# Down-products over a sliding set of eight experts, one shared PSUM rotation, and early low parts on GpSimd

## The chip, the cores and the metric

The kernel runs on one core of one Trainium2 chip. The metric is the device time of one execution in microseconds; lower is better. The time before is the median of three runs.

## What is computed

One residual block on 512 tokens of width 2048, in float32: RMSNorm, two causal attentions (stick-breaking and forgetting) with gated branches and an output projection, then a PEER layer (each token picks, for each of 8 heads, 16 of 16384 single-neuron experts by product keys), then a last RMSNorm. Cut to what matters here:

```python
h = rms_norm(x, norm_ffn_gain)
# expert_ids (t,h,k) and gates (t,h,k) from top-k over two sets of 128 sub-keys
u_sel = expert_u[idb]
act = jax.nn.gelu(jnp.einsum('thkd,td->thk', u_sel, xb))
w = gb * act
v_sel = expert_v[idb]
out = jnp.einsum('thk,thkd->td', w, v_sel)
x = x + out
return rms_norm(x, norm_final_gain)
```

## The kernel before

Matrix products keep float32 accuracy with three passes: `wload` (L96) loads a 128x2048 block of weights in two halves of 512 KB through SP's queue (L104, tile `wr`), ScalarE rounds each half to a high part `wh` (L109), and a low part `wl = wr - wh` is made on VectorE or GpSimd (L111). `mm3` (L117) then issues wh·ah (L118), wh·al (L119) and wl·ah (L120). `wh` and `wl` have three buffers each, `wr` four in the PEER part. From the PEER part on (where the list `more` is not empty) the first half's low part is made on VectorE and the second half's on GpSimd.

The attention part, to about 1335 us of the profile, is not touched. The PEER part treats tokens in two ways. For the last 192 tokens the chosen rows of `expert_u` and `expert_v` are gathered by indirect DMA, 1 MB a gather, by GpSimd's queue (L558), and reduced on VectorE (L565, L574, L582); the tile `row` has three buffers. The other 320 tokens (TD) are dense: the kernel multiplies by all 16384 experts, as 128 blocks of 128, which the code calls experts, and weighs the result with a gate matrix that is zero where an expert was not chosen.

The dense work on one expert c has three parts:

- `expert_up(c)` (L533): 48 matmuls of 320 columns with `uT[c]` into PSUM (`psu`), a scaling on VectorE (L537) and a gelu on ScalarE (L540), giving `gl`.
- `weigh(c)` (L825): `gl` times the gates `gg` of this expert (L830, VectorE), then high part (L833, ScalarE) and low part (L834, VectorE) in `wg`.
- the down-products (L845 to L859): groups of GC = 8 experts. For each of 8 column blocks `jb` a block of `vP` is loaded; each of its two 128-column parts takes 24 matmuls over the eight experts into one PSUM tile (`psy`), which VectorE adds to `acc` (L859).

The stages of this part, by the profile's clock:

- Selection, 1335 to about 2107 us: query projections, top-k on VectorE (`choose`), and the scatter that builds the gate matrix (L796, L801, L803) and stores it to DRAM (`gsp`). In between `early` (L626) runs the first NS = 53 experts' up-products and stores their `gl` to DRAM (`gact_sp`).
- Main, from 2107 us: groups 0 to 15. Experts 0 to 52 are fetched back from `gact_sp` (L815), so groups 0 to 5 have down-products alone; from expert 53 on each group has eight up-products and then its down-products. `gates(grp)` (L818) loads the 20x128 gates of a group's experts from `gsp` to `gg`, which has one buffer (it lies in the unused columns of `h2`).
- End: last norm and the stores.

Gathers are spread by `pace`: every up-product and every down-block counts one unit, and a list `todo` of 388 gathers and small steps is worked off at `rate` of them a unit. PSUM: tag `pu` (2 banks: `psu`, `psq2`), tag `px` (2 banks: `psy`, `psgt` and others), `pr` (4 banks, held by the gathers). The order on each engine is set by a scheduler from the program order and its own costs; it is fixed before the run.

```python
second = more and s == 1
ins = (nc.gpsimd if second else nc.vector).tensor_tensor(lo, raw, hi.bitcast(F32), op=ALU.subtract)
```

Of the kernel before, what the change touches and what calls it, by code (L numbers as in the profile page):

```python
# [18 lines left out]
P = 128  # L19
# [13 lines left out]
NG = NK // GC  # L33
# [10 lines left out]
NS = NH * UPS + TD // TB - -(-(TD // TB) // 3)  # L44
SLOW = 1.1
QROWS = 0.75
LEAD = 1
# [4 lines left out]
def block_kernel(ctx, tc, xT, gains, w_vf, bf, w_qk, w_v, w_g, w_br, w_o, w_q, keysT, uT, vP, expert_u, expert_v, outT):  # L52
# [38 lines left out]
    more = []  # L91
# [4 lines left out]
    def wload(src, between=None, pace=None, units=0.5):  # L96
# [3 lines left out]
        for s in range(2):  # L100
# [9 lines left out]
            second = more and s == 1  # L110
# [381 lines left out]
    pu = pool("pu", 2, space=PSUM)  # L492
    px = pool("px", 2, space=PSUM)
# [39 lines left out]
    def expert_up(c, pace=None):  # L533
        ps = pu.tile([P, T], F32, tag="pu", name="psu")
# [91 lines left out]
    def early(n, pace=None):  # L626
        for _ in range(n):
            if len(started) < NS:
                c = len(started)
                nc.scalar.dma_start(gact_sp[c], expert_up(c, pace))  # L630
                started.append(c)

    with ExitStack() as s1:
# [93 lines left out]
        for h in range(NH):  # L727
            sc = []
            sv = se.tile([P, 2, HT, NK], F32, tag="sv", name="sv")
            for p in range(2):  # L730
# [5 lines left out]
                ps = pu.tile([P, T], F32, tag="pu", name="psq2")  # L736
# [74 lines left out]
    def fetch(c):  # L811
        if c >= NS:
            return expert_up(c, pace)
        g = gl.tile([P, TD], F32, tag="gl", name="gl")
        nc.sync.dma_start(g, gact_sp[c])  # L815
        return g
# [6 lines left out]
    ahead = []  # L823

    def weigh(n):  # L825

        while len(ahead) < min(n + 1 + LEAD, NK):
            ahead.append(fetch(len(ahead)))
        g = ahead[n]
        nc.vector.tensor_tensor(g.rearrange("p (b t) -> p b t", t=TB), g.rearrange("p (b t) -> p b t", t=TB),  # L830
                                gg[:, :, n % GC], op=ALU.mult)
        wg = ex.tile([P, 2, TD], F32R, tag="wg", bufs=GC + 1, name="wg")
# [3 lines left out]

    gates(0)
    ws = [weigh(0)]
    assert len(started) == NS
    rate[0] = len(todo) / (2 * NK - NS - 8)  # L840
    for grp in range(NG):
        first = []
        while len(ws) < GC:
            ws.append(weigh(grp * GC + len(ws)))
        for jb in range(KC // JJ):  # L845
            w = wload(vP[grp, jb])
            if grp + 1 < NG and jb == 1:
                gates(grp + 1)
            if grp + 1 < NG and jb == KC // JJ - 2:
                first.append(weigh((grp + 1) * GC))  # L850
            for jj in range(JJ):
                j = jb * JJ + jj
                ps = px.tile([P, T], F32, tag="px", name="psy")
                for c in range(GC):
                    b = jj * GC + c
                    wh, wl = w[b // 8]
                    cc = slice(b % 8 * P, (b % 8 + 1) * P)
                    mm3(ps[:, :TD], wh[:, cc], wl[:, cc], ws[c][:, 0], ws[c][:, 1], c == 0, c == GC - 1)
# [86 lines left out]
```

## Time and profile before

| what | value |
|---|---|
| median of 3 runs | 3826.57 us (3822.14 to 3833.91) |
| profiled execution, its own time | 3835.57 us |
| its span, first to last instruction | 3833.9 us |
| mean granted TensorE clock | 0.968 |
| PE / PEld busy | 3555.4 us (93%) / 3242.6 us (85%) |
| DVE busy | 2650.1 us (69%) |
| ACT busy | 1274.8 us (33%) |
| POOL busy | 1168.8 us (30%) |
| HBM read, written | 848.69 MB, 35.96 MB |

A busy PE is not PE at its peak: matmuls overlap in the pipeline, so the row of a stretch is read by its number of matmuls as well. The shares are means over stages with different limits; the sections below read the stages apart. 1.7 us of the profiled time lie outside the span.

### The profile page before, as it was taken

How to read it: one execution, taken by the hardware profiler on the slowest of the kernel's cores; microseconds unless marked ns; L12 is line 12 of the kernel's file. 1: busy time of each engine (PE TensorE's matmuls, PEld its weight loads, DVE VectorE, ACT ScalarE, POOL GpSimd, SP SyncE). 2: the span in 40 equal slices, each digit the busy share in tenths (PEclk: the TensorE clock that was granted, in tenths of full speed). 3: DMA queues.
4: the chain of work that ended last, by engine and by line, in shares of the span. 5: the costliest groups of instructions: out<-in, count | busy, mean ns of one | idle time of the engine just before them, and what ended most of it. 6: DMA issues, size and time to landing. Idle time of an engine off the chain costs nothing.

```text
span 3833.9 us, 52828 instructions
## 1 busy us (share of the span) xinstructions
PE 3555.4 (93%) x20665; PEld 3242.6 (85%) x20665; DVE 2650.1 (69%) x3856; ACT 1274.8 (33%) x1798; POOL 1168.8 (30%) x766
## 2 busy tenths in 40 slices
PE   9999999999999999988988888889889999998997
PEld 7888888888887878788978778889889989898997
DVE  5333455434555349999699877788888788778886
ACT  4334222222223223344455322223333333333333
POOL 0000000000000013344522345555555545555552
PEclk9999999999999999998999999999999999999999
DMA  4222222222224236677866899899999999989993
GB/s 144 77 78 77 97 94 97 88 88 78 94 94 137 94 128 228 218 272 264 323 249 236 297 345 337 323 353 360 337 349 358 348 351 367 346 328 347 356 378 133
DMA packets 238249, 888.12 MB, mean 232 GB/s; under 512 B 22696, under 2 KB 79272, under 8 KB 186288
## 3 DMA queue, kind: packets, MB, share of 16 engines
q1 hardware_dynamic: 169792, 447.15, 33.5%
q0 software_dynamic: 58848, 425.75, 28.8%
q10 hardware_dynamic: 9360, 11.83, 0.8%
q8 instruction: 163, 2.67, 0.3%
q14 instruction: 86, 0.70, 0.1%
HBM read 848.69 MB, written 35.96 MB: 231 GB/s over the span
## 4 chain that ended last, share of the span: by engine, by line
PE 61%; DVE 18%; DMA 12%; issue 4%; ACT 2%; POOL 1%; SPq 1%; DVEq 0%; POOLq 0%; ACTq 0%
PE psy L118 5%; PE psy L119 4%; PE psy L120 4%; PE psg L120 3%; PE psg L119 3%; PE psg L118 3%; PE psq L120 3%; PE psq L119 3%; PE psu L120 3%; PE psq L118 3%; DVE wl L111 3%; PE psu L118 3%; PE psu L119 3%; DVE row L565 2%; DMA h<-gsp 2%
## 5 line engine op out<-in xcount | busy, mean ns | idle before, releaser
L109 ACT ACTIVATE wh<-wr 128x1024 fp32r<-128x1024 f32 x768 | 812.4, 1059 | 1919.5 <-PE psy L119 426.5
L111 DVE TENSOR_TENSOR wl<-wr,wh 128x1024 fp32r<-128x1024 f32 x496 | 622.4, 1255 | 457.6 <-ACT wh L109 455.4
L111 POOL TENSOR_TENSOR wl<-wr,wh 128x1024 fp32r<-128x1024 f32 x272 | 658.8, 2422 | 447.9 <-ACT wh L109 348.2
L120 PE MATMUL psu<-h,wl 128*128 128x320 f32 x2048 | 645.8, 316 | 91.2 <-DVE wl L111 91.0
L118 PE MATMUL psy<-wg,wh 128*128 128x320 f32 x2048 | 647.1, 317 | 73.3 <-ACT wg L833 38.1
L120 PE MATMUL psy<-wg,wl 128*128 128x320 f32 x2048 | 645.4, 315 | 15.7 <-DVE wl L111 15.7
L119 PE MATMUL psy<-wg,wh 128*128 128x320 f32 x2048 | 647.0, 316 | 12.3 <-DVE wg L834 12.3
L118 PE MATMUL psu<-h,wh 128*128 128x320 f32 x2048 | 645.8, 315 | 12.5 <-DVE gl L537 7.0
L119 PE MATMUL psu<-h,wh 128*128 128x320 f32 x2048 | 643.3, 314 | 0.0
L120 PEld LDWEIGHTS psu<-h,wl 128*128 128x128 f32 x2048 | 395.2, 193 | 104.8 <-DVE wl L111 104.3
L118 PEld LDWEIGHTS psy<-wg,wh 128*128 128x128 f32 x2048 | 395.0, 193 | 81.6 <-ACT wg L833 39.8
L120 PEld LDWEIGHTS psy<-wg,wl 128*128 128x128 f32 x2048 | 395.8, 193 | 18.5 <-DVE wl L111 18.3
L118 PEld LDWEIGHTS psu<-h,wh 128*128 128x128 f32 x2048 | 395.0, 193 | 18.5 <-ACT wh L109 12.1
L119 PEld LDWEIGHTS psy<-wg,wh 128*128 128x128 f32 x2048 | 395.6, 193 | 15.6 <-DVE wg L834 15.6
L119 PEld LDWEIGHTS psu<-h,wh 128*128 128x128 f32 x2048 | 395.0, 193 | 0.0
L582 DVE SCALAR_TENSOR_TENSOR accg<-row,gact,accg 128x2048 f32<-128x2048 f32 x127 | 298.0, 2347 | 27.3 <-DMA row<-ev,idx 27.0
L565 DVE SCALAR_TENSOR_TENSOR row<-row,rstd_t,h2g 128x2048 f32<-128x2048 f32 x128 | 299.0, 2337 | 10.3 <-DMA row<-eu,idx 10.3
L558 POOL DMA_INDIRECT row<-eu,idx x128 | 159.1, 1243 | 320.2 <-DVE row L565 165.6
L118 PE MATMUL psq<-h,wh 128*128 128x512 f32 x512 | 205.4, 401 | 8.3 <-ACT wh L109 8.3
L558 POOL DMA_INDIRECT row<-ev,idx x128 | 148.7, 1162 | 209.1 <-DVE accg L582 181.7
L119 PE MATMUL psq<-h,wh 128*128 128x512 f32 x512 | 206.2, 403 | 0.4 <-DVE h L169 0.4
L120 PE MATMUL psq<-h,wl 128*128 128x512 f32 x512 | 205.6, 402 | 0.1
(310 smaller groups left out, 6089.1 us busy)
## 6 DMA issues: line engine op xcount, KB each, us to landing
wr<-uT SPq DMA_DIRECT2D x256, 512.0 KB, 6.4
wr<-vP SPq DMA_DIRECT2D x256, 512.0 KB, 7.7
wr<-w_qk SPq DMA_DIRECT2D x64, 512.0 KB, 3.4
wr<-w_g SPq DMA_DIRECT2D x64, 512.0 KB, 3.5
gsp<-st POOLq DMA_DIRECT2D x20, 1024.0 KB, 4.5
wr<-w_br SPq DMA_DIRECT2D x32, 512.0 KB, 3.2
wr<-w_o SPq DMA_DIRECT2D x32, 512.0 KB, 3.1
wr<-w_q SPq DMA_DIRECT2D x32, 512.0 KB, 3.7
```

Of the source, the lines that this page charges most:

```text
L109: nc.scalar.activation(hi, raw, AF.Copy)
L111: ins = (nc.gpsimd if second else nc.vector).tensor_tensor(lo, raw, hi.bitcast(F32), op=ALU.subtract)
L118: nc.tensor.matmul(ps, wh, ah, start=start, stop=False)
L119: nc.tensor.matmul(ps, wh, al, start=False, stop=False)
L120: nc.tensor.matmul(ps, wl, ah, start=False, stop=stop)
L558: nc.gpsimd.indirect_dma_start(out=row.rearrange("p k q -> p (k q)"), out_offset=None, in_=table, in_offset=bass.IndirectOffsetOnAxis(ap=i ...
L565: nc.vector.scalar_tensor_tensor(row, row, rstd_t[:, NT - 1:NT], held[0], op0=ALU.mult, op1=ALU.mult, accum_out=gact[:, i:i + 1])
L582: nc.vector.scalar_tensor_tensor(held[0], row, g[:, i:i + 1], held[0], op0=ALU.mult, op1=ALU.add)
```

## The change

1. Down-products. The set of experts moves on by one per step: step n takes expert n into the set and does one column block, `jb = n % 8`, over experts n-7 to n. Seven steps at the start have sets of 1 to 7 experts, and seven more at the end have 7 to 1. So there are 135 blocks instead of 128, with the same matmuls in all. `vP` is laid out anew: for one `jb` all experts lie behind one another in a partition's row, and a row is 128 KiB long. Within a loaded block the order is expert first, then part: the first half of the block holds four experts with both parts, where before a half held one part for all eight experts.
2. Which experts come early: `EARLY` is 53 of the 128, evenly spread (2, 4, 7, ...), instead of the first 53. In the main stage up-products and fetches so alternate all the way.
3. `LEAD` 1 to 2: an expert is fetched or computed three steps, and weighed two steps, ahead of its first down-block; `wg` has 11 buffers instead of 9. The gates of a group are loaded just before its first expert is weighed.
4. One PSUM rotation: tag `pu` is gone, and all its users share `px`, now with 4 banks.
5. While `sparse[0]` is true (the selection stage), both halves' low parts are made on GpSimd: the 16 blocks of `w_q` and the 53 early experts, 69 low parts in all. In the main stage it is as before.
6. The rate in the main stage is the rest of `todo` over 199 units instead of 195.

```diff
+EARLY = [c for c in range(NK) if (c + 1) * NS // NK > c * NS // NK]
-LEAD = 1
+LEAD = 2
...
-    more = []
+    more, sparse = [], [True]
...
-            second = more and s == 1
+            second = more and (s == 1 or sparse[0])
...
-    pu = pool("pu", 2, space=PSUM)
-    px = pool("px", 2, space=PSUM)
+    px = pool("px", 4, space=PSUM)
...
-                c = len(started)
-                nc.scalar.dma_start(gact_sp[c], expert_up(c, pace))
+                c = EARLY[len(started)]
+                nc.scalar.dma_start(gact_sp[len(started)], expert_up(c, pace))
...
-        if c >= NS:
+        if c not in EARLY:
             return expert_up(c, pace)
         g = gl.tile([P, TD], F32, tag="gl", name="gl")
-        nc.sync.dma_start(g, gact_sp[c])
+        nc.sync.dma_start(g, gact_sp[EARLY.index(c)])
...
-        while len(ahead) < min(n + 1 + LEAD, NK):
-            ahead.append(fetch(len(ahead)))
-        g = ahead[n]
+        g = ahead.pop(n)
...
-        wg = ex.tile([P, 2, TD], F32R, tag="wg", bufs=GC + 1, name="wg")
+        wg = ex.tile([P, 2, TD], F32R, tag="wg", bufs=GC + LEAD + 1, name="wg")
...
+    def down(jb, e0, e1):
+        w = wload(vP[jb, :, e0 * JJ * P:e1 * JJ * P])
+        hb = (e1 - e0) * JJ // 2
+        for jj in range(JJ):
+            j = jb * JJ + jj
+            ps = px.tile([P, T], F32, tag="px", name="psy")
+            for e in range(e0, e1):
+                b = (e - e0) * JJ + jj
+                wh, wl = w[b // hb]
+                cc = slice(b % hb * P, (b % hb + 1) * P)
+                mm3(ps[:, :TD], wh[:, cc], wl[:, cc], ws[e][:, 0], ws[e][:, 1], e == e0, e == e1 - 1)
+            add = nc.vector.tensor_tensor(acc[:, j, :TD], acc[:, j, :TD], ps[:, :TD], op=ALU.add)
+            pace(add, 1.0 / JJ)
+        return add
+    sparse[0] = False
     gates(0)
-    rate[0] = len(todo) / (2 * NK - NS - 8)
-    for grp in range(NG):
...
+    rate[0] = len(todo) / (2 * NK - NS - 4)
+    for n in range(-LEAD, NK):
+        if n + LEAD + 1 < NK:
+            ahead[n + LEAD + 1] = fetch(n + LEAD + 1)
+        if n == -LEAD:
+            ahead[0] = fetch(0)
+        m = n + LEAD
+        if m < NK:
+            if m % GC == 0 and m:
+                gates(m // GC)
+            ws[m] = weigh(m)
+        if n >= 0:
+            add = down(n % GC, max(n - GC + 1, 0), n + 1)
+    for jb in range(GC - 1):
+        add = down(jb, NK - GC + jb + 1, NK)
...
-    out["vP"] = np.asarray(expert_v)[0].reshape(P, NG, GC, KC // JJ, JJ, P).transpose(1, 3, 0, 4, 2, 5).reshape(NG, KC // JJ, P, D)
+    out["vP"] = np.asarray(expert_v)[0].reshape(P, NK, KC // JJ, JJ * P).transpose(2, 0, 1, 3).reshape(KC // JJ, P, NK * JJ * P)
```

How the order on the engines moves, at three places. In the names `wl` is a low part, `row<-eu` a gather, `wr<-vP` and `wr<-uT` half a block of weights, `gl<-gact_sp` a fetch of a stored expert; the numbers are those of the program's tiles.

GpSimd, among the up-products of the selection stage, before:

```order
L558 DMA row_13318<-eu,idx_9642 128x2048
L111 TENSOR_TENSOR wl_13197<-wr_13194,wh_13196 128x1024
L558 DMA row_13386<-eu,idx_9642 128x2048
L111 TENSOR_TENSOR wl_13265<-wr_13262,wh_13264 128x1024
L558 DMA row_13488<-eu,idx_9642 128x2048
L111 TENSOR_TENSOR wl_13333<-wr_13330,wh_13332 128x1024
```

The same place now:

```order
L111 TENSOR_TENSOR wl_12263<-wr_12260,wh_12262 128x1024
L111 TENSOR_TENSOR wl_12325<-wr_12322,wh_12324 128x1024
L557 DMA row_12452<-eu,idx_9639 128x2048
L111 TENSOR_TENSOR wl_12331<-wr_12328,wh_12330 128x1024
L111 TENSOR_TENSOR wl_12393<-wr_12390,wh_12392 128x1024
L557 DMA row_12520<-eu,idx_9639 128x2048
```

Between two gathers GpSimd now makes two low parts, the second half of one expert and the first half of the next, instead of one.

VectorE, at the start of the second group of the main stage, before (`wg` is the low part in `weigh`, `gl<-gl,h2` the weighing with the gates):

```order
L830 TENSOR_TENSOR gl_17155<-gl_17155,h2_8494 128x320
L830 TENSOR_TENSOR gl_17590<-gl_17590,h2_8494 128x320
L830 TENSOR_TENSOR gl_17721<-gl_17721,h2_8494 128x320
L834 TENSOR_TENSOR wg_17593<-gl_17155,wg_17593 128x320
L830 TENSOR_TENSOR gl_17727<-gl_17727,h2_8494 128x320
L859 TENSOR_TENSOR acc_79<-acc_79,psy_17342 128x320
```

In the main stage now, the weighing of one stored expert (`gl_22534`) and of one just computed (`gl_22671`):

```order
L827 TENSOR_TENSOR gl_22534<-gl_22534,h2_8494 128x320
L111 TENSOR_TENSOR wl_22684<-wr_22681,wh_22683 128x1024
L592 TENSOR_TENSOR gact_b_9643<-gact_b_9643,ggate_b_9644 128x64
L831 TENSOR_TENSOR wg_22678<-gl_22534,wg_22678 128x320
L536 TENSOR_TENSOR gl_22671<-psu_22607,rstd_77 128x320
L581 SCALAR_TENSOR_TENSOR accg_22503<-row_22673,gact_9640,accg_22503 128x2048
L111 TENSOR_TENSOR wl_22755<-wr_22752,wh_22754 128x1024
L846 TENSOR_TENSOR acc_79<-acc_79,psy_22693 128x320
L581 SCALAR_TENSOR_TENSOR accg_22503<-row_22719,gact_9640,accg_22503 128x2048
L827 TENSOR_TENSOR gl_22671<-gl_22671,h2_8494 128x320
```

The weighings of a group, which stood in bunches, now stand one by one between the other work.

SP's queue in a group of down-products alone, before:

```order
L104 DMA wr_18043<-vP 128x1024
L104 DMA wr_18049<-vP 128x1024
L104 DMA wr_18110<-vP 128x1024
L815 DMA gl_18335<-gact_sp_9653 128x320
L104 DMA wr_18116<-vP 128x1024
L104 DMA wr_18180<-vP 128x1024
```

In the main stage now:

```order
L104 DMA wr_21596<-uT 128x1024
L814 DMA gl_21519<-gact_sp_9650 128x320
L104 DMA wr_21605<-uT 128x1024
L104 DMA wr_21669<-vP 128x1024
L104 DMA wr_21675<-vP 128x1024
L104 DMA wr_21742<-vP 128x1024
L104 DMA wr_21748<-vP 128x1024
L104 DMA wr_21813<-uT 128x1024
```

An expert's two halves of `uT` now stand between one or two blocks of `vP` throughout. Where there are two blocks, a down-block follows a down-block on PE; that is so for 53 of the 128 steps and in the seven at the end.

## Rows read from the trace of the kernel before

**Rows 1.** The page, part 2: 40 slices, busy share in tenths.

```profile
DVE  5333455434555349999699877788888788778886
DMA  4222222222224236677866899899999999989993
```

**Rows 2.** Stages: length, busy us (instructions) by engine, granted clock, DMA share, GB/s.

```profile
1335.00:2107.00 772.00, 695.97 (x4092) 635.65 (x4090) 656.54 (x1771) 320.88 (x507) 265.56 (x162) 0.94 0.67 238
2107.00:2574.00 467.00, 395.58 (x2522) 384.11 (x2523) 373.31 (x481) 140.53 (x168) 223.71 (x131) 0.93 0.89 331
2574.00:2806.00 232.00, 211.42 (x1383) 207.50 (x1382) 190.34 (x191) 70.96 (x84) 123.57 (x75) 0.97 0.93 347
2806.00:3707.00 901.00, 823.61 (x5414) 810.86 (x5413) 735.86 (x579) 283.86 (x343) 481.78 (x294) 0.97 0.94 352
```

**Rows 3.** The same view, two stretches of 100 us.

```profile
2900.00:3000.00 100.00, 94.23 (x638) 92.69 (x637) 84.37 (x65) 32.16 (x40) 54.12 (x34) 1.00 0.98 373
3700.00:3800.00 100.00, 96.11 (x651) 95.48 (x651) 78.35 (x73) 43.81 (x59) 41.36 (x21) 0.98 0.61 224
```

**Rows 4.** Waits of PE, 1335 to 2107: total us, times, longest.

```profile
PE psu L120 <- DVE wl L111: 31.4, 15, 5.0
```

**Rows 5.** Instruction groups, 1900 to 2107: busy us, mean ns, idle before.

```profile
L801 DVE TENSOR_SCALAR ab<-i,ia,gt 128x128 f32<-128x128 f32 x274 | 96.0, 412 | 0.0
...
L111 POOL TENSOR_TENSOR wl<-wr,wh 128x1024 fp32r<-128x1024 f32 x15 | 35.8, 2384 | 10.1 <-ACT wh L109 9.9
```

**Rows 6.** Instruction groups over the whole span, same columns.

```profile
L109 ACT ACTIVATE wh<-wr 128x1024 fp32r<-128x1024 f32 x768 | 812.4, 1059 | 1919.5 <-PE psy L119 426.5 <-PE psu L119 299.2 <-PE psg L119 271.4
L111 POOL TENSOR_TENSOR wl<-wr,wh 128x1024 fp32r<-128x1024 f32 x272 | 658.8, 2422 | 447.9 <-ACT wh L109 348.2 <-DMA h<-gsp 55.4 <-ACT f L667 15.1
...
L111 DVE TENSOR_TENSOR wl<-wr,wh 128x1024 fp32r<-128x1024 f32 x496 | 622.4, 1255 | 457.6 <-ACT wh L109 455.4
...
L834 DVE TENSOR_TENSOR wg<-gl,wg 128x320 fp32r<-128x320 f32 x128 | 145.6, 1150 | 12.3 <-ACT wg L833 11.9
...
L859 DVE TENSOR_TENSOR acc<-acc,psy 128x320 f32<-128x320 f32 x256 | 122.7, 480 | 75.2 <-PE psy L120 75.0
```

**Rows 7.** VectorE, then GpSimd in time, 2104 to 2110: start, us, instruction.

```profile
2104.76 3.92 DVE L801 TENSOR_SCALAR ab<-i,ia,gt 128x128 f32<-128x128 f32 x4
2109.21 1.10 DVE L801 TENSOR_SCALAR ab<-i,ia,gt 128x128 f32<-128x128 f32 x4
...
2104.49 1.21 POOL L558 DMA_INDIRECT row<-eu,idx  x1 [0.30 <-DVE gl L537]
2105.72 2.35 POOL L111 TENSOR_TENSOR wl<-wr,wh 128x1024 fp32r<-128x1024 f32 x1
```

**Rows 8.** Chain of waits, 2107 to 2574; VectorE's wait from 2218.

```profile
by line: DMA gl<-gact_sp 17.3%; PE psy L118 10.9%; PE psy L120 10.6%; PE psy L119 10.6%; DMA row<-eu,idx 8.2%; DMA row<-eu,idx_b 6.3%; issue 5.5%; DVE row L565 4.9%; DVE ab L801 3.6%; DVE wl L111 3.3%; DMA h<-gsp 3.2%; POOL wl L111 2.4%; DV
...
2230.81 13.80 DMA gl<-gact_sp
2356.60 12.01 DMA gl<-gact_sp
...
DVE gl L830 <- DMA gl<-gact_sp: 39.3, 11, 8.3
```

**Rows 9.** Waits of PE and GpSimd, 2806 to 3707.

```profile
PE psy L118 <- DVE acc L859: 7.4, 5, 3.5
...
POOL row L558 <- DVE accg L582: 256.4, 97, 9.5
POOL wl L111 <- ACT wh L109: 123.7, 64, 12.6
```

**Rows 10.** The page, part 3; VectorE's wait for gates, whole span.

```profile
q1 hardware_dynamic: 169792, 447.15, 33.5%
q0 software_dynamic: 58848, 425.75, 28.8%
...
DVE gl L830 <- DMA h<-gsp: 53.5, 10, 8.5
```

More of the change, by code (lines that the diff above doesn't have):

```diff
@@ L32 @@
 GC = 8
-NG = NK // GC
 JJ = D // (GC * P)
@@ L533, in expert_up @@
     def expert_up(c, pace=None):
-        ps = pu.tile([P, T], F32, tag="pu", name="psu")
+        ps = px.tile([P, T], F32, tag="px", name="psu")
         proj(ps[:, :TD], wload(uT[c], pace=pace), h2, n=TD)
@@ L735, in block_kernel @@
                     token_rows(lambda k: acc[:, k, T - P:], "h2g")
-                ps = pu.tile([P, T], F32, tag="pu", name="psq2")
+                ps = px.tile([P, T], F32, tag="px", name="psq2")
                 proj(ps, wload(w_q[b], pace=qpace if b > 4 else None, units=2.0), h2)
@@ L821, in gates @@
             nc.sync.dma_start(gg[:, b:e], gsp[:, b:e, grp * GC:(grp + 1) * GC])
-    ahead = []
+    ahead = {}
     def weigh(n):
-        while len(ahead) < min(n + 1 + LEAD, NK):
-            ahead.append(fetch(len(ahead)))
-        g = ahead[n]
+        g = ahead.pop(n)
         nc.vector.tensor_tensor(g.rearrange("p (b t) -> p b t", t=TB), g.rearrange("p (b t) -> p b t", t=TB),
                                 gg[:, :, n % GC], op=ALU.mult)
-        wg = ex.tile([P, 2, TD], F32R, tag="wg", bufs=GC + 1, name="wg")
+        wg = ex.tile([P, 2, TD], F32R, tag="wg", bufs=GC + LEAD + 1, name="wg")
         nc.scalar.activation(wg[:, 0], g, AF.Copy)
@@ L835, in weigh @@
         return wg
+    def down(jb, e0, e1):
[12 more added lines that the diff above has]
+        return add
+    ws = {}
+    sparse[0] = False
     gates(0)
-    ws = [weigh(0)]
     assert len(started) == NS
-    rate[0] = len(todo) / (2 * NK - NS - 8)
-    for grp in range(NG):
[L842 to L858, printed above, removed]
-                add = nc.vector.tensor_tensor(acc[:, j, :TD], acc[:, j, :TD], ps[:, :TD], op=ALU.add)
-                pace(add, 1.0 / JJ)
-        ws = first
+    rate[0] = len(todo) / (2 * NK - NS - 4)
[13 more added lines that the diff above has]
+        add = down(jb, NK - GC + jb + 1, NK)
     while todo:
@@ L878, in block_kernel @@
         nc.scalar.activation(acc[:, j], acc[:, j], AF.Copy, scale=gain[j])
-    ps = pu.tile([P, NT, 2], F32, tag="pu", name="psn3")
+    ps = px.tile([P, NT, 2], F32, tag="px", name="psn3")
     for t in range(NT):
@@ L886, in block_kernel @@
                             sm[:, 3].unsqueeze(2).to_broadcast([P, NT, P]), op=ALU.mult)
-    psr = pu.tile([P, T], F32, tag="pu", name="psr")
+    psr = px.tile([P, T], F32, tag="px", name="psr")
     nc.tensor.matmul(psr, ones, fin[1][:, 1], start=True, stop=True)
```

## The prediction

> **What bounds the kernel now.** I read the page's slices first, then the busy time by stage, then in each stage the waits, the instruction groups and the chain of waits. In the slices [rows 1] VectorE is full only in slices 16 to 19 and in 21 and 22 of 40: that is the selection stage. DMA is at 0.8 or more from slice 24 on: that is the main stage. The attention part before it is not touched by the change and drops out.
>
> The stages [rows 2] are read by matmuls per time. In the steady part of the main stage 5414 matmuls take 901 us, 166 ns each, so a block of 48 takes 8.0 us, with DMA busy for 0.94 of the time at 352 GB/s. In 3700 to 3800, where the gathers have run out, 651 matmuls lie in 96.1 us busy, 148 ns each, 7.1 us a block [rows 3]. So PE has some 0.9 us a block to spare there, and gathers, weights and VectorE's queue together take it. From 2107 to 2574, the start and the groups that have down-products alone, 2522 matmuls take 467 us: 185 ns each, at only 331 GB/s. That is the slowest part of the main stage, although PE, VectorE and DMA are all below full. The chain of waits says why [rows 8]: 17.3% of it, some 81 us of 467, are landings of stored experts (`gl<-gact_sp`, single ones of 12 to 14 us), and VectorE itself stood for them for 39.3 us. They come in bunches, just before they are weighed. In selection VectorE is busy for 656.5 of 772 us, and PE stands 31.4 us for a low part that VectorE had not made yet [rows 2, 4].
>
> **The change, part by part.** The sum is made against the profiled execution, 3835.57 us, which lies 9.0 us above the median of 3826.57; I carry the same difference over to the median.
>
> *Low parts to GpSimd (A).* 69 low parts leave VectorE, 1255 ns each, 86.6 us; GpSimd gets 69 x 2.42 = 167 us [rows 6] on top of 265.6 busy in selection [rows 2], 433 of 772, so there is room on average. But VectorE does not keep all of it. While GpSimd makes a low part, four gate instructions of VectorE (L801) took 3.92 us, and the next four, with GpSimd idle, 1.10 [rows 7]. So each low part on GpSimd holds VectorE up, if VectorE is at such an instruction. How much? In the scatter, L801 was busy 96.0 us for 274, against 274 x 0.275 = 75.4 undisturbed: 20.6 us for 15 low parts, 1.4 us each [rows 5]. Over the main stage the wg subtraction takes 1150 ns where an add of the same shape that reads PSUM takes 480 [rows 6]: 128 x 0.67 = 86 us for the 272 - 69 = 203 low parts there, 0.42 each. Selection is a mix of scatter and top-k, nearer the scatter; I take 1.0. A = -69 x (1.255 - 1.0) = -18 us, between -58 (0.42) and +10 (1.4). I do not add the 31.4 us of rows 4: while VectorE is full they are the same time. The Trainium skill (SBUF — State Buffer, Who interferes with whom) says that VectorE instructions with two SBUF inputs, and copies or tensor_scalars in a fast mode, share a port pair with GpSimd, and that the second to start "fully blocks" until the first is done. Rows 7 agree. By that rule a moved low part can cost VectorE up to 2.42 us, more than the 1.255 it saves; that is a rival below.
>
> *Stored experts spread, LEAD 2, sets that move on (B).* The fetches of 53 stored experts now come one at a time, three steps ahead (the order on SP and VectorE shows it), and up- and down-products alternate from the start, so the stretch 2107 to 2574 should run like the later one. At 166 ns its 2522 matmuls take 420 us instead of 467: -47. By bytes it gains less: 331 GB/s x 467 us = 154.6 MB, at 352 GB/s 439 us: -28, since no byte is saved. The waits in the chain (81 us) are nearer the first. I take -42, between -48 and 0 (nothing, if the bytes set it after all).
>
> *One PSUM rotation (C).* PE waited 7.4 us for an add to free a bank in 901 us [rows 9]; over the 1133 us from 2574 that is -9, between -9 and 0. `psu` and `psy` now wait in one ring of four; a late gelu scaling could hold back a `psy`, but it is 0.48 us of work.
>
> *Halves that hold four experts (D).* This is a new wait. Before, the first half's buffers were free after 24 matmuls, and the second half was first read at the 25th. Now each part reads both halves: the first half is held for 36 of 48 matmuls and the second needed from the 13th. With three buffers, where a down-block follows a down-block, the second half's rounding can start only 24 matmuls (3.55 us) before it is needed, instead of 48 (7.1 us). It takes 1.06 on ScalarE and 2.42 on GpSimd [rows 6], 3.48 together: just in time if GpSimd is free. In 64 of 112 cases (seven groups of sixteen blocks) it was free and waiting for ScalarE [rows 9]; in the other 43% something, mostly a gather of 1.21 us [rows 7], stood in front. 60 such steps (53 and 7 at the end) x 0.43 x (1.21 - 0.9, the pace's spare) = 8; I take +10. Bounds: 0, and 60 x 2.6 = 158 if every one finds a gather that itself waits for its row (256.4 us in 97) [rows 9].
>
> *Edges and the rest (E).* Seven more blocks: 14 more adds of 0.48 us [rows 6], 6.7 us on VectorE, and short blocks at both ends: +7, between 0 and 14. The rate (199 for 195) moves 2% of the gathers a little later: nothing, hidden in the same main stage. Gates: VectorE waited for them 53.5 us in 10 of 16 fills [rows 10]. They are now asked for nearer to the weighing in the program, but on VectorE about as much work as before, some 10 us, stands between the last reader and the next; I take 0, between -25 and +25.
>
> *The new layout of vP.* Same bytes, runs of 4 KB, but 128 KiB apart. The nearest row is the gathers: rows of 8 KB from anywhere [rows 10], 28.8% of the engines' time for 425.75 MB, against 33.5% for 447.15 MB in the other queue. Scattered addresses are no dearer per byte: 0. The Trainium skill (DMA: Bandwidth & Descriptors, Latency and other measured facts) gives 207 GB/s for a row pitch of 512 KiB and 103 for 4 MiB, against 214 when padded; 128 KiB is not listed, and the rule's 3% on the 128 MB of vP at 352 GB/s would be an estimated +12 us. No row here shows it.
>
> Sum: -18 - 42 - 9 + 10 + 7 = -52. 3835.6 - 52 = 3783.6 for a run like the profiled one, **3775 us for the median**.
>
> **The rivals.**
> - *Bytes set the main stage.* DMA at 0.94 busy for it [rows 2]; then B and C are nothing, and A, D and E cancel: 3826. Against it: 373 GB/s in a stretch of 100 us [rows 3].
> - *The main stage gains everywhere.* Up- and down-products mixed evenly keep all queues full, and PE runs at 160 ns: 9319 matmuls from 2107 to 3707 take 1491 us, not 1600, -109 in place of B and C; 3716. For: every unit gets the same load. Against: 552 MB would need 370 GB/s throughout, which only the best stretches have.
> - *Slower: the second half comes late (D).* GpSimd's queue is in order; if a gather in front waits for its row, half the way to the upper bound, +80 in place of +10: -52 + 70 = +18, and at the upper bound +96. I take +35: 3862. It decides from about 1.2 us per such step ((52 + 10 + 12) / 60). Against: GpSimd was idle before most of its low parts.
> - *Slower: GpSimd holds VectorE up in selection (A).* At the full 2.42 us per moved low part A is +80, the sum +46: 3873. It decides from 1.75 us per low part, where A outweighs the other terms' -34. Against: 1.4 was the worst seen.
>
> **How the numbers follow.** A measurement of this kernel can tell about 0.3%, 11.5 us, from no change. Forecast (3738 to 3815) 0.55; bytes, no change 0.13; gain everywhere (under 3738) 0.15; late halves 0.09; VectorE held up 0.08. Faster 0.70, same 0.13, slower 0.17. The range 3700 to 3840 takes in the forecast's case, no change, and the nearer half of the gain everywhere; it leaves out the slower cases and the far gains, some 2 in 10. The likeliest case's own range is 3738 to 3815.
>
> **What would show it.** Right: selection shorter by some 18 us, with PE's waits for a VectorE low part there gone and L801 dearer; 2107 to 2574 replaced by a stretch at about 166 ns a matmul, no `gl<-gact_sp` among the long pieces of the chain, DMA above 350 GB/s from the start; almost no PE wait for an add. PE waiting for a GpSimd low part, which the profile before does not have, is D; up to 30 us fits. Wrong: selection not shorter with VectorE as busy as before (A); the main stage at the same GB/s and time (bytes); GpSimd's low parts ahead of every other releaser of PE (D).

## The result and the profile after

The change made the kernel slower. Its median is 3878.32 us (four runs, 3876.39 to 3885.91), that of the kernel before on the same chip 3828.85 us; the ratio is 1.0134, 95% interval 1.0112 to 1.0156, some 50 us. The forecast was 3775, range 3700 to 3840: wrong in sign, and outside its range. The profiled execution took 3877.51 us for a span of 3875.8. Its slices, as [rows 1]:

```profile
DVE  5333455435555458697477787788887888777875
DMA  4222222222224247257975799999999999988993
```

Of the six slices in which VectorE was full before (16 to 19 and 21, 22) only slice 18 still is, and the DMA engines are busy from slice 24 on as before: VectorE was relieved, and the time grew.

I cut both traces at the last scatter product (`psgt`), which starts at 2138 us before and at 2190 after, and at equal lengths behind it. First the kernel after (columns as in [rows 2]):

```profile
1335.00:2190.00 855.00, 728.51 (x4229) 663.96 (x4228) 619.10 (x1767) 329.19 (x517) 425.09 (x236) 0.94 0.63 225
2190.00:2626.00 436.00, 388.22 (x2512) 380.36 (x2511) 348.59 (x399) 137.39 (x171) 221.20 (x140) 0.95 0.91 342
2626.00:3759.00 1133.00, 1032.01 (x6772) 1015.54 (x6772) 894.04 (x808) 360.55 (x428) 605.09 (x362) 0.96 0.93 354
```

and the kernel before, cut in the same way:

```profile
1335.00:2138.00 803.00, 721.24 (x4264) 659.74 (x4263) 687.54 (x1836) 335.50 (x522) 274.69 (x168) 0.94 0.67 240
2138.00:2574.00 436.00, 370.31 (x2352) 360.01 (x2351) 342.31 (x417) 125.92 (x154) 214.57 (x124) 0.93 0.90 333
2574.00:3707.00 1133.00, 1035.03 (x6795) 1018.36 (x6794) 926.21 (x769) 354.82 (x426) 605.35 (x368) 0.97 0.93 351
```

The selection stage became 52 us longer, although VectorE is busy for 68 us less in it. The first 436 us of the main stage hold 2512 matmuls in place of 2352 (174 ns each for 185), which is the stretch that B was meant for; the next 1133 us hold as many as before, not more. From the last scatter product to the last down-product the main stage takes 1659 us for 1673, so half of what the start gained is lost again. So the profiles say +52 in selection, -14 in the main stage, +4 at the end.

**Selection.** PE's waits from 1372 (before: 1373) to the last scatter product; columns: total us, times, longest. After:

```profile
PE psgt L802 <- DVE ab L800: 40.9, 42, 3.3
PE pss L743 <- ACT q L738: 31.0, 14, 8.7
PE psu L120 <- POOL wl L111: 29.0, 16, 3.4
PE psrep L763 <- DVE rep L757: 12.2, 1, 12.2
```

Before:

```profile
PE psu L120 <- DVE wl L111: 32.1, 16, 5.0
PE psgt L803 <- DVE ab L801: 28.5, 19, 2.5
PE psrep L764 <- DVE rep L758: 4.8, 1, 4.8
```

The wait for a low part that I saw in [rows 4] has only changed its engine. New is PE waiting for ScalarE's copy of the query (`q`) before the scores `pss`. The same moment in both traces shows why. Before, the scores of one block stand some matmuls inside the next block of `psq`, and PE goes on:

```profile
1447.78 0.40 PE L118 MATMUL psq<-h,wh 128*128 128x512 f32 x1
1448.02 1.12 PE L744 MATMUL pss<-kt,q 128*128 128x128 f32 x8
1448.89 0.48 PE L119 MATMUL psq<-h,wh 128*128 128x512 f32 x1
```

After, they stand right behind their own block (PE's rows, then ScalarE's):

```profile
1447.52 0.40 PE L120 MATMUL psq<-h,wl 128*128 128x512 f32 x1
1456.66 2.08 PE L743 MATMUL pss<-kt,q 128*128 128x128 f32 x8 [8.74 <-ACT q L738]
1458.96 0.63 PE L119 MATMUL psq<-h,wh 128*128 128x512 f32 x1
...
1455.26 0.40 ACT L712 ACTIVATE gt<-tv,nm,rstd_t 128x16 f32<-128x16 f32 x1 [3.28 <-DVE nm L709]
1456.04 0.58 ACT L738 ACTIVATE q<-psq 128x512 f32<-128x512 f32 x1
```

In ScalarE's queue the copy stands behind a softmax step of the top-k (`gt`), which waits for VectorE. All three engines stand in one line here.

**Main stage.** VectorE's and PE's waits of the kernel after, 2190 to 3850:

```profile
DVE gl L827 <- DMA h<-gsp: 94.0, 12, 11.2
DVE gl L827 <- DMA gl<-gact_sp: 54.5, 17, 6.8
PE psy L120 <- DVE wl L111: 102.2, 30, 9.1
PE psy L120 <- POOL wl L111: 15.8, 25, 1.9
```

PE's waits for VectorE's low part before, 2138 to 3812:

```profile
PE psu L120 <- DVE wl L111: 59.0, 32, 4.4
PE psy L120 <- DVE wl L111: 15.7, 10, 3.9
```

Before, VectorE stood 53.5 us for gates [rows 10] and, over the whole main stage, 40.8 us for stored experts. Both grew: B spread the fetches, and over this stage they are no earlier than before. PE's wait for VectorE's low part, 74.7 us before and mostly in up-products, is now mostly in down-products and somewhat longer. One fill of gates (SyncE's rows, then VectorE's; `L820` asks for the gates):

```profile
2367.89 5.43 SPq L820 DMA_DIRECT2D h<-gsp  x3
2373.43 6.13 SPq L104 DMA_DIRECT2D wr<-vP  x2
...
2375.79 0.47 DVE L846 TENSOR_TENSOR acc<-acc,psy 128x320 f32<-128x320 f32 x1
2384.63 0.49 DVE L827 TENSOR_TENSOR gl<-gl,h 128x320 f32<-128x320 f32 x1 [8.37 <-DMA h<-gsp]
```

The fill is issued when the last reader of the old gates is done (2367.86) and lands over 16 us later. The weighing that needs it is the next one in program, so VectorE stands in front of it, and behind it in VectorE's queue stand low parts for which PE waits (102.2 us in all; how much of it the gates cause is not shown by these rows). In the chain of waits, 2190 to 3850, such landings are 9.1%; in that of the kernel before, 2138 to 3812, they are 5.3% (the kernel after first):

```profile
by line: issue 9.6%; PE psy L120 9.4%; DMA h<-gsp 9.1%; PE psy L118 8.6%; PE psy L119 8.5%; DVE wl L111 5.7%; DMA gl<-gact_sp 5.5%; POOL wl L111 3.7%; DVE accg L581 3.7%; DMA row<-ev,idx 3.6%; DMA row<-eu,idx_b 3.1%; SPq L820 3.0%; PE psu L
by line: PE psy L118 10.4%; PE psy L119 10.2%; PE psy L120 10.1%; issue 8.2%; DMA h<-gsp 5.3%; DMA gl<-gact_sp 4.8%; DVE wg L834 4.6%; DMA row<-ev,idx 4.5%; PE psu L120 3.9%; DMA row<-ev,idx_b 3.7%; PE psu L118 3.6%; PE psu L119 3.5%; DVE w
```

### The profile page after: what moved, and what is told of

Its sections match the earlier page's. It is cut to its first block, busy times and chain, and to the rows that moved or that the text cites. A ratio compares the mean times of both kernels' runs of the same rounds, so it can differ in the third digit from the quotient of the medians.

```text
span 3875.8 us, 52647 instructions
## 1 busy us (share of the span) xinstructions
PE 3563.5 (92%) x20665; PEld 3249.3 (84%) x20665; DVE 2541.5 (66%) x3808; ACT 1280.1 (33%) x1808; POOL 1315.6 (34%) x842
## 4 chain that ended last, share of the span: by engine, by line
PE 58%; DVE 16%; DMA 13%; issue 6%; POOL 3%; ACT 2%; SPq 1%; POOLq 0%; DVEq 0%; ACTq 0%
PE psy L120 4%; DMA h<-gsp 4%; PE psy L118 4%; PE psy L119 4%; PE psg L120 3%; PE psg L119 3%; PE psg L118 3%; PE psu L119 3%; PE psu L118 3%; PE psu L120 3%; DVE wl L111 3%; PE psq L119 2%; PE psq L120 2%; POOL wl L111 2%; PE psq L118 2%
## 5 line engine op out<-in xcount | busy, mean ns | idle before, releaser
L109 ACT ACTIVATE wh<-wr 128x1024 fp32r<-128x1024 f32 (+1 forms) x782 | 814.9, 1044 | 1786.0 <-PE psu L119 409.4
L111 POOL TENSOR_TENSOR wl<-wr,wh 128x1024 fp32r<-128x1024 f32 (+3 forms) x348 | 830.0, 2387 | 640.9 <-ACT wh L109 604.7
L111 DVE TENSOR_TENSOR wl<-wr,wh 128x1024 fp32r<-128x1024 f32 (+2 forms) x434 | 550.6, 1269 | 407.7 <-ACT wh L109 404.0
L120 PE MATMUL psy<-wg,wl 128*128 128x320 f32 x2048 | 656.3, 321 | 118.7 <-DVE wl L111 102.2
L118 PE MATMUL psu<-h,wh 128*128 128x320 f32 x2048 | 642.3, 314 | 11.3 <-ACT wh L109 9.5
L120 PE MATMUL psg<-h,wl 128*128 128x512 f32 x512 | 203.4, 397 | 0.0
```

Of the source, the lines that this page charges most:

```text
L109: nc.scalar.activation(hi, raw, AF.Copy)
L118: nc.tensor.matmul(ps, wh, ah, start=start, stop=False)
L120: nc.tensor.matmul(ps, wl, ah, start=False, stop=stop)
```

## The experiments

Theory 1: the common rotation changes PE's order in selection, and that costs the time. Theory 2: low parts on GpSimd cost the selection stage more than VectorE saves. Theory 3: the main stage gained little because gates and stored experts land late. Against 3 stands "bytes set the main stage". Each ratio is to the kernel before on the same chip. "Selection" is from the last attention product to the last scatter product, "main" from there to the last down-product, in the profiled execution.

| run | median us | ratio (95%) | selection | main |
|---|---|---|---|---|
| before | 3828.85 | | 766 | 1673 |
| after | 3878.32 | 1.0134 (1.0112, 1.0156) | 818 | 1659 |
| e3_b_onering | 3878.85 | 1.0133 (1.0089, 1.0178) | 785 | 1690 |
| e4_b_pool | 3844.03 | 1.0046 (1.0026, 1.0066) | 776 | 1670 |
| e1_split | 3844.40 | 1.0035 (1.0018, 1.0051) | 782 | 1665 |
| e2_nosparse | 3840.13 | 1.0034 (1.0019, 1.0048) | 784 | 1653 |
| e5_main_alone | 3822.33 | 0.9992 (0.9979, 1.0006) | 766 | 1654 |
| e6_gates_act | 3840.00 | 1.0037 (1.0020, 1.0053) | 766 | 1678 |
| e7_gates_fetch_act | 3852.22 | 1.0055 (1.0036, 1.0075) | 765 | 1689 |
| e8_four_banks_main | 3857.46 | 1.0085 (1.0060, 1.0111) | 766 | 1679 |
| e9_gates_three_ahead | 3780.69 | 0.9872 (0.9848, 0.9897) | 766 | 1622 |
| e10_fetch_too | 3759.02 | 0.9819 (0.9796, 0.9842) | 766 | 1601 |
| e11_no_refills | 3744.80 | 0.9781 (0.9756, 0.9805) | 766 | 1587 |
| e12_all_four_banks | 3763.16 | 0.9828 (0.9805, 0.9852) | 766 | 1597 |
| e13_after_early_gates | 3806.19 | 0.9943 (0.9921, 0.9966) | 819 | 1585 |
| e14_b_fetch_two_ahead | 3834.54 | 1.0023 (1.0008, 1.0038) | 766 | 1670 |

**Selection: one part at a time.** In e1_split the changed kernel gets its two rings back (`psq2`, `psn3` and `psr` go the same way):

```diff
-    px = pool("px", 4, space=PSUM)
+    pu = pool("pu", 2, space=PSUM)
+    px = pool("px", 2, space=PSUM)
...
-        ps = px.tile([P, T], F32, tag="px", name="psu")
+        ps = pu.tile([P, T], F32, tag="pu", name="psu")
```

> The changed kernel with the two PSUM rotations of before (psu and psq2 on two banks, psy, psgt, pss on two others). Theory 1 (the common rotation costs the query stage): the scores (pss) stand inside the next query block again, PE's wait for ScalarE's copy of q (31.0 us) goes, the last query product ends near 1580 us instead of 1616, the last scatter product near 2140 instead of 2190; time 3878 - 45 = about 3833, less if the main stage does not miss the four banks. Theory 2 (low parts on GpSimd cost the query stage): query stage as in the changed kernel, time 3870 to 3885.

e2_nosparse keeps the one rotation and leaves the first half's low parts on VectorE until the main stage:

```diff
-    more, sparse = [], [True]
+    more, sparse = [], [False]
```

> The changed kernel with the first half's low part on VectorE in the selection stage too, as before. Theory 1: query stage as long as in the changed kernel (to about 1616 us), and the 18 us that I predicted from the moved low parts are lost: 3880 to 3900. Theory 2: query stage back to about 1580 us, time about 3840.

e3_b_onering is the kernel before with the first edit reversed:

> The kernel before with nothing changed but the one PSUM rotation of four banks. Theory 1: it alone makes the query and scatter stages some 45 to 50 us longer, and the main stage some 10 to 25 us shorter (PE's 24.7 us of waits for an add): 3829 + 25 to 40 = 3855 to 3870. Theory 2: 3829 or a little less.

e4_b_pool is the kernel before with the low parts of both halves on GpSimd in selection:

```diff
-            second = more and s == 1
+            second = more and (s == 1 or sparse[0])
...
+    sparse[0] = False
     gates(0)
```

> The kernel before with nothing changed but both low parts on GpSimd in selection. Theory 1: my term A, 18 us faster, about 3811 (3771 to 3840 by its bounds). Theory 2: slower by some 40 us, about 3869, all of it in the query stage.

Both edits cost time, and neither is the whole loss. The rotation costs the kernel before 49 us, more than the 25 to 40 expected: by the profile 19 in selection and 17 in its main stage, where a gain of 10 to 25 had been expected. Why its main stage lost is open. The low parts cost 14 by the medians and 18 by the ratio, where theory 2 said 40; undoing either of them in the changed kernel gives back 34 to 38 (theory 1 had 45 for e1_split; e2_nosparse came out where theory 2 had it). Together they lengthen selection by 52 us, alone by 19 and 11.

I cut selection once more, at the last query product (`psq`). From the last attention product to there it is 207 us before, 226 with either edit alone (e3_b_onering, e4_b_pool) and 244 with both: in the query part the two add up. So does the wait for the query copy. With the rotation alone it is short each time (PE's waits of e2_nosparse, 1372 to 1616),

```profile
PE pss L743 <- ACT q L738: 19.9, 14, 1.4
```

with the low parts alone there are three (PE's waits of e4_b_pool, 1371 to 1617),

```profile
PE pss L744 <- ACT q L739: 11.3, 3, 6.1
```

and with both it is 31.0 us, the sum of the two, up to 8.7 at a time. For the rotation this wait is as long as the query part grew, which bears theory 1 out; for the low parts it is 11.3 us of 19, and another 5 are PE's busy time, at a granted clock of 0.95 for 0.98.

What the two cost beyond their sum lies behind the last query product, up to the last scatter product (columns as in [rows 2]; before, e3_b_onering, e4_b_pool, after):

```profile
1579.80:2138.40 558.60, 482.37 (x3195) 467.80 (x3194) 511.30 (x1227) 263.56 (x365) 213.53 (x130) 0.93 0.74 266
1598.70:2157.70 559.00, 474.54 (x3157) 460.48 (x3156) 490.44 (x1227) 262.11 (x364) 211.21 (x128) 0.95 0.73 263
1597.00:2147.60 550.60, 478.72 (x3205) 463.71 (x3203) 463.38 (x1165) 263.49 (x366) 319.67 (x175) 0.96 0.73 258
1615.90:2189.50 573.60, 483.05 (x3157) 468.25 (x3156) 433.86 (x1167) 256.96 (x360) 317.68 (x176) 0.93 0.69 249
```

Alone the rotation changes this part by nothing and the low parts shorten it by 8 us; together they lengthen it by 15, and by 19 in e13_after_early_gates, which has the same two edits. Of the 23 us beyond the sum some 12 are PE's busy time, at a lower granted clock (0.93 for 0.95 and 0.96), and the rest is waiting. Why the two together do this is open.

In e4_b_pool VectorE did get lighter in selection, 642.93 us busy for 687.54, and selection took 11 us longer:

```profile
1335.00:2148.00 813.00, 721.80 (x4272) 658.48 (x4270) 642.93 (x1764) 336.01 (x523) 429.04 (x235) 0.96 0.67 236
```

but it then stood for gathered rows (the last columns of this instruction group, 1371 to 2148: 22.8 us idle, waiting for the gather; 0.0 in the kernel before):

```profile
L565 DVE SCALAR_TENSOR_TENSOR row<-row,rstd_t,h2g 128x2048 f32<-128x2048 f32 x74 | 172.6, 2337 | 22.8 <-DMA row<-eu,idx 22.6
```

e5_main_alone makes both edits, of e1_split and of e2_nosparse:

> The changed kernel with two PSUM rings of two as before and with VectorE making the first half's low parts in the selection stage as before: steps C and A both undone, what is left is the reworked main stage (stored experts spread, sets that move on, halves of four experts). Theory 'selection': the selection stage ends again some 766 us after the attention part, as before, and the main stage takes about 1665 us as in e1_split, so the time is 3815 to 3830, some 50 to 60 us under the changed kernel and 0 to 15 us under the kernel before. Rival 'the main stage itself lost': then it stays at 3835 to 3850 and the selection stage of the two earlier variants was not the place. In both cases B (-42) is not there in full: VectorE's waits for gates should still be near 95 us.

As expected: selection is as long as before, to the microsecond, and the time lies in the range named. So the two edits are the whole loss there: 3878.32 - 3822.33 = 56 us. What is left, the reworked main stage, is worth nothing that the runs can tell from zero (0.9992); its profile says 19 us, which lies within the spread of the runs.

**The main stage: what is late.** e6_gates_act asks for the next gates right behind the weighing that last reads the old ones, on ScalarE's queue:

```diff
-            if m % GC == 0 and m:
-                gates(m // GC)
             ws[m] = weigh(m)
+            if (m + 1) % GC == 0 and m + 1 < NK:
+                gates((m + 1) // GC)
...
-            nc.sync.dma_start(gg[:, b:e], gsp
+            (nc.scalar if grp else nc.sync).dma_start(gg[:, b:e], gsp
```

> e5_main_alone, with the eight experts' gates asked for right behind the last weighing that reads the old ones, on ScalarE's DMA queue, in place of just ahead of the next weighing on SyncE's, where the weights stand ahead of them. Same bytes, same work. Theory 'late gates eat what the sets and the spreading gained': VectorE's waits for gates fall from about 95 us to under 30, PE's waits for VectorE's low part and add (65 and 61 us in e1_split) to about half, and the time falls by 20 to 50 us against e5_main_alone. Rival 'bytes set the main stage': the waits move to weights or gathers, DMA stays at 340 GB/s, and the time is within 6 us of e5_main_alone.

A miss: slower by 18 us, and VectorE still waits 85.1 us for gates, where under 30 had been expected. One fill in ScalarE's rows in time,

```profile
2314.46 9.13 ACTq L821 DMA_DIRECT2D h<-gsp  x3
2323.69 2.00 ACT L109 ACTIVATE wh<-wr 128x1024 fp32r<-128x1024 f32 x2 [8.76 <-issue]
```

and ScalarE's waits from 2138 to 3816, of which this is one:

```profile
ACT wh L109 <- issue: 114.3, 24, 10.9
```

That wait is 4.1 us in e5_main_alone. Issuing the three DMAs of a fill takes some 5 to 13 us here, and on ScalarE that time is taken from the high parts. The Trainium skill (DMA: Bandwidth & Descriptors, Issuing engines are not separate DMA queues) says that a second issuing engine saves only the time on the sequencer to initiate the DMA, "usually small". The trace agrees that nothing landed earlier (medians of 14.4 and 17.6 us for the two sizes of a fill's DMAs, 11.1 and 15.2 in e5_main_alone), but here that time was not small, 114.3 us, and it fell on an engine that had other work. The run moves the request and changes the queue at once; what the earlier request alone is worth on SyncE's queue it does not show.

e7_gates_fetch_act moves the stored experts' fetches to that queue as well (`nc.sync` to `nc.scalar` in `fetch`), and e8_four_banks_main adds that up- and down-products take the banks of both rings in turn in the main stage:

> e6_gates_act, with the fetches of the 53 stored experts on ScalarE's DMA queue too, in place of SyncE's. Theory 'what comes late on VectorE comes late because it stands behind weights in one queue': VectorE's waits for stored experts fall from about 55 us to under 20, and the time by another 5 to 20 us against e6_gates_act. Rival 'the fetch is late because it is asked for only one step ahead': the waits stay and the time is within 6 us. A loss would be ScalarE held up by a fetch that waits for its buffer: then PE's waits for ScalarE's high part (wh) grow.

> e7_gates_fetch_act, with the products of the main stage taking the four banks of the two rings in turn (up- and down-products alike), while the selection stage keeps two rings of two. Theory 'one rotation helps the main stage and hurts only the selection stage': as e2_nosparse took 1653 us in the main stage where e1_split took 1665, the time falls by 5 to 15 us against e7_gates_fetch_act, PE's wait for the add (61 us in e1_split) is nearly gone, and the selection stage keeps its length. Rival: with the gates in time the add is in time too, and it changes nothing (within 5 us).

Misses too: 12 us slower, and another 5 us slower with ranges that overlap. The waits for stored experts stayed (54.6 us in e5_main_alone, 50.1 in e6_gates_act, 54.3 in e7_gates_fetch_act), and four banks took PE's wait for the add (34.2 us in e7_gates_fetch_act) away without any gain in time.

So the lead had to come from the program. e9_gates_three_ahead is e5_main_alone with twelve places for gates in columns that lie unused beside them, and the next eight asked for three steps ahead, on SyncE's queue:

```diff
+GS = 12
...
-            nc.sync.dma_start(gg[:, b:e], gsp[:, b:e, grp * GC:(grp + 1) * GC])
+            for c in range(grp * GC, (grp + 1) * GC, GC // 2 if grp * GC % GS > GS - GC else GC):
+                w = GC // 2 if grp * GC % GS > GS - GC else GC
+                nc.sync.dma_start(gg[:, b:e, c % GS:c % GS + w], gsp[:, b:e, c:c + w])
...
-                                gg[:, :, n % GC], op=ALU.mult)
+                                gg[:, :, n % GS], op=ALU.mult)
...
-            if m % GC == 0 and m:
-                gates(m // GC)
             ws[m] = weigh(m)
+            if m % GC == 5 and m + 3 < NK:
+                gates(m // GC + 1)
```

> e5_main_alone, with room for twelve experts' gates in place of eight and the next eight asked for three steps ahead of their first use, on SyncE's queue as before. Same bytes. Theory 'late gates': VectorE's waits for gates (96 us in e5_main_alone) fall under 10 us, PE's waits for VectorE's low part and add (64 and 59 us) to half or less, and the time falls by 20 to 60 us against e5_main_alone. Rival 'bytes set the main stage': the waits go to weights and gathers, and the time is within 8 us of e5_main_alone.

e10_fetch_too also fetches a stored expert two steps ahead:

```diff
-        if n + LEAD + 1 < NK:
-            ahead[n + LEAD + 1] = fetch(n + LEAD + 1)
+        for c in (n + LEAD + 2, n + LEAD + 1):
+            if c < NK and c not in ahead and (c in EARLY or c == n + LEAD + 1):
+                ahead[c] = fetch(c)
```

> e9_gates_three_ahead, with each stored expert fetched two steps ahead of its weighing in place of one. Theory 'late landings': VectorE's waits for stored experts (55 us) fall under 15 us and the time by another 5 to 25 us against e9_gates_three_ahead. Rival 'bytes': within 6 us, and the waits turn into waits for gathers or weights.

e11_no_refills is e5_main_alone without the two lines that ask for the next gates (it leaves out the refills, so its output is not the block's and only its time counts), and e12_all_four_banks adds the banks in turn to e10_fetch_too:

> e5_main_alone with the refills of the gates left out: the first eight experts' gates are used for all 128, so 15 of 16 fills, about 19.7 MB, are not read and their waits are gone. Theory 'late gates': the same as e9_gates_three_ahead within 10 us, since what costs is the wait and not the bytes. Rival 'bytes': e9_gates_three_ahead gains nothing and this one gains up to 19.7 MB at 341 GB/s, 58 us, against e5_main_alone. If both bear, it lies under e9_gates_three_ahead by some part of 58 us.

> e10_fetch_too, with the products of the main stage taking four banks in turn, the selection stage keeping two rings of two. Theory 'one rotation helps the main stage': another 5 to 15 us under e10_fetch_too, PE's wait for the add nearly gone. Rival: within 5 us of e10_fetch_too, since adds that are not held up come in time. If the theory of late landings holds in full, this is the fastest of all, 3750 to 3790.

e9_gates_three_ahead gains 42 us with the same bytes: theory 3, as far as the gates go. In e5_main_alone VectorE's wait for them (2138 to 3792) was

```profile
DVE gl L828 <- DMA h<-gsp: 95.8, 13, 11.8
```

and none is left among VectorE's waits; its wait for stored experts grew from 54.6 to 83.0 us. PE's waits for the add and for VectorE's low part go from 58.9 and 63.7 us to

```profile
PE psy L119 <- DVE acc L850: 39.8, 19, 5.4
PE psy L121 <- DVE wl L112: 33.4, 26, 3.9
```

so the low part's is halved, as expected, and the add's falls by a third only. e10_fetch_too gains another 22, as forecast, but not for the reason given: VectorE waits for stored experts as long as in e9_gates_three_ahead (83.0 us in 20), where under 15 had been expected. SyncE's rows show why: in each of the 16 waits of e10_fetch_too the fetch was issued only 7 to 16 us before VectorE went on, much as before. Asked for a step earlier in the program, it was not issued earlier in time. What fell is its `wg` subtraction, which by [rows 6] takes longer than the 480 ns of an add of its shape; that GpSimd's low parts hold it up is my reading there, not shown. The group's row of e9_gates_three_ahead,

```profile
L835 DVE TENSOR_TENSOR wg<-gl,wg 128x320 fp32r<-128x320 f32 x128 | 112.5, 880 | 29.9 <-ACT wg L834 29.9
```

VectorE's wait in e10_fetch_too,

```profile
DVE gl L831 <- DMA gl<-gact_sp: 81.3, 16, 7.3
```

the same group in it,

```profile
L835 DVE TENSOR_TENSOR wg<-gl,wg 128x320 fp32r<-128x320 f32 x128 | 70.8, 560 | 8.3 <-ACT wg L834 8.2
```

and a steady stretch of it. Why the other lead shortens the subtractions is open, and with it why the 22 us were gained.

```profile
2700.00:3600.00 900.00, 843.88 (x5589) 830.25 (x5588) 716.84 (x647) 296.87 (x352) 504.35 (x298) 0.98 0.97 366
```

At 161 ns a matmul and 366 GB/s it is past the 352 GB/s that I took for full [rows 2]. Without the refills' 19.7 MB the time is another 36 us under e9_gates_three_ahead, where 58 were the most that bytes were expected to give. So a fill costs time even where nothing waits for it. That may be its bytes, or SyncE's time to issue it (up to 10.9 us for the three DMAs of one in e9_gates_three_ahead) ahead of the weights in its queue; the two were not tried apart. e12_all_four_banks is no faster than e10_fetch_too, where 5 to 15 us had been hoped for.

e13_after_early_gates puts the edits of e9_gates_three_ahead and e10_fetch_too into the changed kernel as it is, and e14_b_fetch_two_ahead sets `LEAD = 2` in the kernel before:

> The changed kernel with its one rotation and its low parts on GpSimd kept, and only the two edits of e9_gates_three_ahead and e10_fetch_too made: gates three steps ahead in twelve slots, stored experts two steps ahead. Theory 'two separate losses' (selection lost 56 us, late landings cost 63 us, and neither has to do with the other): 3878 - 63 = 3815, between 3805 and 3825, with the selection stage as long as in the changed kernel (818 us from the attention part's end). Rival 'one loss seen twice' (a selection stage that ends late leaves gathers behind and so makes the main stage late): then the time falls by less than 45 us, to over 3833.

> The kernel before with one number changed: a stored expert (and any other) is fetched or computed two weighings ahead in place of one. Theory 'the lead of B, not the spreading, is what the stretch with stored experts needs': VectorE's waits for stored experts (41 us) fall under 15 us and the time by 10 to 25 us. Rival 'the stretch is slow because the stored experts come in bunches and no up-products stand between': within 8 us of the kernel before, with the stretch from 2138 to 2574 still near 185 ns a matmul.

e13_after_early_gates lies at 3806.19, 72 us under the changed kernel (I had 63), with selection still at 819: two separate causes. e14_b_fetch_two_ahead is not faster (1.0023), VectorE's wait for stored experts stays at 40.3 us (40.8 before), where under 15 had been expected, and its first 436 us hold 2372 matmuls, 184 ns each: the earlier fetch alone does not help the stretch that B was after. So its 174 ns come from the spreading, the moving set, the earlier weighing or the new layout; these were not tried apart.

e10_fetch_too beats both kernels: 1.8% under the kernel before, 119 us under the change.

## Why the prediction was wrong

The forecast's sum was -52 us; by the profiles it is +42. Of the 94 us between, 70 lie in selection (+52 for -18), 20 in the main stage (-14 for -34) and 4 at the end. Two steps failed above all: A, that less work for VectorE makes selection shorter, and C, that the common rotation changes nothing in selection.

- **A (-18) fell.** By the busy rows each of the 69 moved low parts gave VectorE 44.6 / 69 = 0.65 us, so it was held up for some 0.61 us of 1.255 (an estimate), not 1.0. The size was wrong in my favour; the step that failed is "VectorE is full ... that is the selection stage", taken to mean that VectorE's work sets the stage's length. In e4_b_pool it had 44.6 us less to do, and selection took 11 us longer. In the query part, up to the last `psq` product, its busy time did not even fall (168.3 us for 164.6): 17 low parts of 21.6 us are gone, but four more gathers are reduced there, 9.4 us, and the rest of its work took longer. Meanwhile PE stood 11.3 us for query copies, which it had not done before. That product moved from 1580 to 1597 us; the rest of the stage won back 8.
- **C (-9) fell by most.** I counted only waits for a free bank, in the main stage, and of what the ring holds back only the 0.48 us of a gelu scaling; its worth in selection I put at nothing. Alone it cost 19 us there, all of it in the query part, and 17 in the main stage of the kernel before. What a common ring changes is the order: the scores no longer stand inside the next query block. (That the ring hands out its tiles as the program names them, and so forces this order, is my reading.) In the main stage the wait for the add did go, as forecast, and the time did not follow (e12_all_four_banks against e10_fetch_too).
- **B (-42) was over-sized.** At the start it gave 2512 x (185 - 174) ns = 28 us, near the byte figure that I set aside, though at 342 GB/s and not at the 352 of that figure; in the later stretch it gave nothing, and of the 28 the whole main stage keeps 14.
- **E, "gates: I take 0", was too low.** I had seen that they are asked for nearer to their use and priced this by the work on VectorE in between. The price is the landing: over 16 us for the fill shown, with one weighing in between. VectorE's wait went from 53.5 to 94.0 us. In e9_gates_three_ahead taking away 95.8 us of it was worth 42 us of time, so the 40.5 more cost perhaps 18, an estimate that lies inside E's range of 25.
- **D (+10)** fits as a wait: PE waited 15.8 us for a GpSimd low part of a down-product, in 25 waits of at most 1.9 us, and the upper bound of 158 was far off. What it costs in time was not tried by itself.
- **The layout of vP (0)** was not tried by itself. The halves of vP land in 7.3 us (e5_main_alone, median) for 7.7 before, and e10_fetch_too moves 366 GB/s with it. No run here shows the loss that the prediction estimated from the Trainium skill's figures for row pitch (DMA: Bandwidth & Descriptors, Latency and other measured facts).
- **Rivals.** "Bytes" fell as the account of the main stage with e9_gates_three_ahead, which moves the same bytes. "VectorE held up" gave 3873, near the time measured, by a hold of 2.42 us that no run shows: luck. "Late halves" fell with D. What turned the sign was in none of them: the query part, 37 us longer, half of it by the order on PE, and 15 us behind it that only the two edits together cost. The order of PE's instructions shows the first of these, and my working drew on that of GpSimd, VectorE and SyncE alone.

## What to carry to other kernels

Joining two PSUM rings into one is a change of order, not only of room: look where PE's instructions go before pricing any wait. A transfer that an in-order engine waits for has to be issued ahead of its need by more than its measured landing. Here another issuing engine gave no such lead, and asking earlier in the program gave it to the gates but not to the stored experts: look at the time of the issue, not only at the program. A high busy share does not make an engine the bound of a stage: ask what it waits for in turn, and what waits for it. And two edits that each cost little can cost more together, so try them alone and together, stage by stage.

## What the runs showed of the hardware that was not expected

After standing for 8.74 us PE ran at half its clock: in the first row below (the changed kernel, just behind the wait shown above) the granted clock is 0.50, its level of 1.2 GHz, and twelve matmuls take 4 us; in the second it is 1.00, and sixteen take 3.4. So this wait cost some 1.5 us more than its length: 12 matmuls, 333 ns each in place of 212.

```profile
1458.40:1462.40 4.00, 4.00 (x12) 3.13 (x12) 4.00 (x14) 0.86 (x5) 1.23 (x2) 0.50 0.98 406
1462.60:1466.00 3.40, 3.40 (x16) 2.72 (x15) 3.40 (x14) 0.08 (x1) 0.00 (x0) 1.00 0.92 366
```

A fill of gates, 1.3 MB in rows of 512 bytes, kept SyncE for 5 to 14 us in the changed kernel's main stage, and it landed later than weights: the median landing in e5_main_alone is 11.1 and 15.2 us for its parts (512 and 256 KB), 7.3 for half a block of vP (512 KB).
